# S5 preparation in a hybrid decoder trunk: C A^k B of four groups as four matmuls on column strips, one copy out, D added in one operation

## The chip, the cores and the metric

The kernel runs on one NeuronCore of a Trainium2 chip. The metric is the device time of one execution in microseconds (us), lower is better. TensorE (PE, its weight loads PEld), VectorE (DVE), ScalarE (ACT) and GpSimd (POOL) each work through their own instruction list in order; SyncE (SP) issues all transfers of this kernel, also in order.

## The reference, cut to what matters

Two layers over 512 tokens of width 1024. Each layer runs three token mixers on one input projection: Mamba-2 SSD (A), an S5 state space model (B) and latent attention, MLA (C). The change lies in B. S5 splits 1024 channels into 64 groups of 16 channels, each with 64 complex states:

```
bu = einsum('gph,bsgh->bsgp', bb, uf)          # input to states
x_t = abar * x_(t-1) + bu_t                    # diagonal, per group
y = Re(einsum('ghp,bsgp->bsgh', c, x)) + d_skip * uf
```

The kernel works in chunks of 8 tokens. Within a chunk y is a convolution of u with the 16x16 matrices C A^k B, k = 0 to 7, of each group, with the diagonal D added at k = 0.

## The kernel before, in words

Per layer, `layer` projects the input, then opens the pool `prep` and starts `s5_prep`, a generator. `mla` advances it by `fill` calls between its heads, so that S5 preparation (in lines: projections of u, powers of A, products) is spread over the 16 attention heads. After that come the S5 scan, SSD, the S5 blocks, the three merges and the output projection. A scheduler of the language puts each engine's instructions in order when the program is built, by times it assumes; the order is then fixed.

The head of `s5_prep` loads parameters and computes powers A^0 to A^8 (`ar`, `ai`) in many DVE operations on 128x64. It also loads D as `dT` (16 rows by 64 groups) and writes zeros to the first 112 columns of `kpad`, a buffer in DRAM which later holds the convolution matrices in a Toeplitz layout. `block(b)` handles eight groups: projection of u, a detour of u through DRAM (`ud`, eight `puf` transfers), loads of B and C (`bc`), then `q1` (name `pq`, on DVE) and the scaled B (`bb`, in the zero padded tile `pbb`) on POOL. `front` computes on POOL, for two groups, `w1` (name `pw`) and `v1` (name `pv1`, in a buffer of four groups, two buffers in all) and stores `v1` to `odr`. `back` runs one step behind: it transposes `w1` on PE into `pm`, splits that on ACT and DVE, and multiplies with u into `pM`. Every second step closes four groups:

- `pk`: one f32 matmul, B of four groups (4 x 32 columns, 16 of each 32 in use) as stationary operand, `v1` of the same four groups (4 x 128 columns) as moving operand. Of the 4 x 4 blocks of the result only the diagonal ones are used.
- four ACT copies of one 16x128 block each into `kf` (name `pkf`), rows 0 to 15.
- on POOL, `dd` (name `pdd`) = identity times `dT`, then `kf` += `dd` on 16 columns of each group.
- one transfer of `kf` into `kpad`.

There are 16 such closings per layer, 32 in all. The tiles `pm` and `pk` share one PSUM bank (tag `pb`).

Of the kernel before, what the change touches and what calls it, by code (L numbers as in the profile page):

```python
# [9 lines left out]
F32 = mybir.dt.float32  # L10
# [3 lines left out]
ALU = mybir.AluOpType  # L14
# [6 lines left out]
P = 128  # L21
# [13 lines left out]
class Trunk:  # L35
# [109 lines left out]
    def constants2(self):  # L145
        nc, c = self.nc, self.const
        for name, n in (("sgn", 2), ("ones", P), ("utri", P), ("cosT", 512), ("sinT", 512), ("cmask", 512)):
            t = c.tile([P, n], F32, name=name)
            nc.sync.dma_start(t, self.a[name])
            setattr(self, name, t)  # L150
        self.sel = c.tile([64, 16], F32R, name="sel")
        self.tt(self.sel, self.ident[0:64, 0:16], self.ident[0:64, 32:48], ALU.add)

# [81 lines left out]
    def s5_prep(self, l, pp):  # L235
        nc, a = self.nc, self.a
        pt = lambda nm, shape, bufs=1: pp.tile(shape, F32, name=nm, tag=nm, bufs=bufs)
# [46 lines left out]
        for h in range(2):  # L284
            q, g = slice(64 * h, 64 * h + 64), slice(32 * h, 32 * h + 32)
# [1 line left out]
            nc.vector.tensor_copy(sc1[q, 1], ar[q, 8, g])  # L287
            self.ts(sc2[q, 0], ai[q, 8, g], -1.0, None, ALU.mult)
            nc.vector.tensor_copy(sc2[q, 1], ai[q, 8, g])
        dT = pt("dT", [16, 64])  # L290
        nc.sync.dma_start(dT, a["s5_dT"][l])
        zero = pp.tile([16, 112], F32, name="zero", tag="pkf")
        nc.vector.memset(zero, 0.0)
        d = lambda nm, shape: self.dr.tile(shape, F32, name=f"{nm}{l}")
        kpad, odr, msd, u2 = d("kpad", [16, 64, 240]), d("odr", [P, 64, P]), d("msd", [2, 64, 2, 32, 64]), d("u2", [8, P, 512])
# [5 lines left out]
        et = self.gt  # L301
        pf = lambda nm: pp.tile([P, 512], F32, name=nm, tag="pf", bufs=2)

        bbp = [pt(f"pbb{i}", [P, 8, 32]) for i in range(2)]
# [54 lines left out]
        def back(b, s, uf, bb, v1, w1):  # L359
            if s == 0:  # L360
                u = keep["u"] = pp.tile([P, 8, 2, 64], F32R, name="pu2", tag="pu2")
                self.split(uf.rearrange("p (g c) -> p g c", g=8), u[:, :, 0], u[:, :, 1])
                keep["mo"] = pf("pmo").rearrange("p (g c) -> p g c", g=8)
                nc.gpsimd.memset(keep["mo"][:, :, 0], 0.0)
            u, mo = keep["u"], keep["mo"]
            pm = self.pq.tile([P, 512], F32, name="pm", tag="pb")
            for i in range(NB):
                nc.tensor.transpose(pm[:, i * P:i * P + P], w1[:, i].rearrange("p k h -> p (k h)"), self.ident)
            mh, ml = (pp.tile([P, NB * P], F32R, name=x, tag=x) for x in ("pmh", "pml"))
            self.split(pm[:, :NB * P], mh, ml)  # L370
            if s % 2 == 0:
                keep["pM"] = self.pq.tile([P, 4, 2, 64], F32, name="pM", tag="pM")
            pM = keep["pM"]
            for i in range(NB):
                g = NB * s + i
                k = slice(i * P, (i + 1) * P)
                nc.tensor.matmul(pM[:, g % 4], mh[:, k], u[:, g], start=True, stop=False)
                nc.tensor.matmul(pM[:, g % 4, 0], ml[:, k], u[:, g, 0], start=False, stop=True)
            if s % 2:
                q = 4 * (s // 2)  # L380
                self.act_(mo[:, q:q + 4, 1:64], pM[:, :, 0, 0:63])
                self.tt(mo[:, q:q + 4, 1:64], mo[:, q:q + 4, 1:64], pM[:, :, 1, 0:63], ALU.add)

                pk = self.pq.tile([P, 4, P], F32, name="pk", tag="pb")
                nc.tensor.matmul(  # L385
                    pk.rearrange("p g k -> p (g k)"), bbp[b % 2][:, q:q + 4].rearrange("p g h -> p (g h)"),
                    v1[:, :, 0:8].rearrange("p g k h -> p g (k h)"), start=True, stop=True,
                )
                kf = pt("pkf", [16, 4, P])
                for i in range(4):  # L390
                    self.act_(kf[:, i], pk[32 * i:32 * i + 16, i])
                g4 = slice(8 * b + q, 8 * b + q + 4)
                dd = pt("pdd", [16, 4, 16])
                et(
                    dd, self.ident[0:16, 0:16].unsqueeze(1).broadcast_to([16, 4, 16]),
                    dT[:, g4].unsqueeze(2).broadcast_to([16, 4, 16]), ALU.mult,
                )
                et(kf[:, :, 0:16], kf[:, :, 0:16], dd, ALU.add)
                nc.sync.dma_start(kpad[:, g4, 112:240], kf)
            if s == 3:  # L400
                nc.sync.dma_start(msd[b // 4, :, :, 8 * (b % 4):8 * (b % 4) + 8].rearrange("p r g c -> r p g c"), mo)

        todo = None
        for b in range(8):
            blk = block(b)
            yield
            for s in range(4):
                vw = front(b, s, *blk)
                if todo:
                    back(*todo)  # L410
                todo = (b, s, blk[0], blk[1], *vw)
                yield
        back(*todo)


# [811 lines left out]
```

## Time and profile before

| | |
|---|---|
| median of 3 runs | 2001.6 us (2001.11 to 2006.5) |
| the profiled execution | 1999.34 us, its span 1997.5 us |
| MLA with S5 preparation, layers 1 and 2 | about 90 to 400 us and 1080 to 1385 us |
| head of the preparation | about 20 to 90 us and 1019 to 1080 us |
| busy: PE, DVE, ACT, POOL | 1883.4, 1448.1, 941.1, 645.6 us |
| `pk` on PE | 64 MATMUL instructions for 32 calls, first at 91.4, last at 1375.8 us |

A chain is the sequence of work that ended last, followed back from the end; a share of it says where shorter work could shorten the run. A median duration of a PE matmul includes the flight through the array, so matmuls overlap in the list; the chain counts each only for the time until the next one follows.

### The profile page before, as it was taken

To read this page: it belongs to the slowest core of one execution; us is meant where nothing else is said; L and a number is where in the kernel's file an instruction comes from. 1 tells how busy PE (TensorE), PEld (TensorE's weight loads), DVE (VectorE), ACT (ScalarE), POOL (GpSimd) and SP (SyncE) were. 2 spreads that over 40 slices of the span, in tenths; PEclk is the share of its full clock that TensorE was granted. 3 is DMA by queue.
4 is the path that set the end of the run, shared out by engine and by line. 5 is a ranking of instruction groups with operands and counts; after the bars stand their busy time and mean duration, and the time that the engine had idled before them with its cause. 6 is when DMAs were issued, how large, how long until landed. Compare 5 with 4: busy or idle time off the path is not lost.

```text
span 1997.5 us, 27806 instructions
## 1 busy us (share of the span) xinstructions
PE 1883.4 (94%) x9688; PEld 1530.5 (77%) x9688; DVE 1448.1 (72%) x2845; ACT 941.1 (47%) x1743; POOL 645.6 (32%) x743
## 2 busy tenths in 40 slices
PE   7897999899999989999998999998999999999998
PEld 5685777687887778888876777776878887788887
DVE  6866667699999857744579666677999996666443
ACT  4364556522555545543333655564235563555431
POOL 1855467301233201201118556672013331012010
PEclk9898999899999999999998999998999999899999
DMA  5333244232312266345223333342232224662541
GB/s 159 94 115 86 88 116 121 74 120 81 131 64 73 70 172 182 106 132 177 96 84 88 112 104 111 91 140 83 96 122 78 75 74 111 182 173 85 166 130 42
DMA packets 132605, 219.96 MB, mean 110 GB/s; under 512 B 36208, under 2 KB 75760, under 8 KB 131952
## 3 DMA queue, kind: packets, MB, share of 16 engines
q1 hardware_dynamic: 132464, 218.19, 36.0%
q8 instruction: 76, 1.25, 0.2%
q14 instruction: 65, 0.53, 0.1%
HBM read 182.08 MB, written 31.33 MB: 107 GB/s over the span
## 4 chain that ended last, share of the span: by engine, by line
PE 59%; DVE 24%; DMA 8%; POOL 3%; ACT 3%; issue 2%; SPq 1%; DVEq 0%; POOLq 0%; ACTq 0%
PE mm L116 13%; PE mm L117 13%; PE mm L119 12%; DVE wl L78 4%; DMA wf<-in_w_in 3%; DVE keep L69 3%; PE mm L61 2%; PE mm L62 2%; PE mm L63 2%; DVE ms L894 2%; DVE sc_t L891 2%; PE pk L385 2%; DVE ms L893 1%; PE aux L61 1%; PE aux L62 1%
## 5 line engine op out<-in xcount | busy, mean ns | idle before, releaser
L116 PE MATMUL mm<-hh,wh 128*128 128x512 f32 (+1 forms) x1232 | 500.9, 407 | 16.0 <-DVE ql L78 8.8
L117 PE MATMUL mm<-hl,wh 128*128 128x512 f32 (+1 forms) x1232 | 493.5, 401 | 0.0
L66 ACT ACTIVATE wh<-wf 128x1024 fp32r<-128x1024 f32 (+1 forms) x294 | 291.4, 994 | 422.9 <-PE mm L117 232.7
L78 DVE TENSOR_TENSOR wl<-wf,wh 128x1024 fp32r<-128x1024 f32 (+1 forms) x243 | 297.0, 1227 | 180.6 <-ACT wh L66 151.9
L119 PE MATMUL mm<-hh,wl 128*128 128x512 f32 (+1 forms) x1232 | 315.4, 393 | 3.8 <-DVE wl L78 3.8
L116 PEld LDWEIGHTS mm<-hh,wh 128*128 128x128 f32 (+1 forms) x1232 | 237.3, 193 | 77.9 <-DVE ql L78 9.9
L117 PEld LDWEIGHTS mm<-hl,wh 128*128 128x128 f32 (+1 forms) x1232 | 236.7, 192 | 50.0 <-issue 1.9
L119 PEld LDWEIGHTS mm<-hh,wl 128*128 128x128 f32 (+1 forms) x1232 | 227.7, 187 | 53.3 <-DVE wl L78 4.6
L81 POOL TENSOR_TENSOR mg<-mg,tmp 128x512 f32<-128x512 f32 x32 | 77.4, 2420 | 461.4 <-DVE tmp L78 244.0
L81 POOL TENSOR_TENSOR wl<-wf,wh 128x1024 fp32r<-128x1024 f32 (+1 forms) x51 | 109.0, 2138 | 291.2 <-PE mm L119 185.9
L116 PE MATMUL mm<-ah,wh 128*128 128x512 f32 x512 | 200.6, 394 | 0.0
L117 PE MATMUL mm<-al,wh 128*128 128x512 f32 x512 | 199.8, 391 | 0.0
L119 PE MATMUL mm<-ah,wl 128*128 128x512 f32 x512 | 127.6, 390 | 0.0
L116 PEld LDWEIGHTS mm<-ah,wh 128*128 128x128 f32 x512 | 96.5, 189 | 21.6 <-issue 1.8
L117 PEld LDWEIGHTS mm<-al,wh 128*128 128x128 f32 x512 | 96.3, 188 | 20.6 <-DVE keep L78 0.5
L119 PEld LDWEIGHTS mm<-ah,wl 128*128 128x128 f32 x512 | 95.7, 188 | 19.5
L612 DVE CUSTOM_DVE_ANT_0 sc<-aux,cmask 128x128 f32<-128x128 f32 (+3 forms) x128 | 60.3, 485 | 50.2 <-PE aux L63 48.4
L81 POOL TENSOR_TENSOR pv<-pq,ar 128x288 f32<-128x288 f32 x64 | 56.7, 906 | 86.3 <-PE pk L385 69.8
L66 ACT ACTIVATE sc<-sc,nm 128x128 f32<-128x128 f32 (+3 forms) x128 | 70.3, 553 | 28.7 <-DVE nm L73 28.7
L78 DVE TENSOR_TENSOR pl<-aux,ph 128x512 fp32r<-128x512 f32 (+1 forms) x96 | 54.7, 593 | 25.6 <-ACT ph L66 25.2
L69 DVE SCALAR_TENSOR_TENSOR keep<-mm,cw,keep 128x511 f32<-128x511 f32 (+2 forms) x96 | 71.0, 740 | 2.1 <-ACT keep L66 1.5
L66 ACT ACTIVATE tmp<-mm 128x512 f32<-128x512 f32 x76 | 44.8, 593 | 58.5 <-PE mm L63 32.3
(344 smaller groups left out, 4083.4 us busy)
## 6 DMA issues: line engine op xcount, KB each, us to landing
wf<-in_w_in SPq DMA_DIRECT2D x156, 512.0 KB
odr<-pv SPq DMA_DIRECT2D x64, 128.0 KB
wf<-in_w_c SPq DMA_DIRECT2D x16, 512.0 KB
wf<-in_w_a SPq DMA_DIRECT2D x16, 512.0 KB
wf<-kpad SPq DMA_DIRECT2D x128, 64.0 KB
wf<-odr SPq DMA_DIRECT2D x16, 512.0 KB
wf<-in_w_glu SPq DMA_DIRECT2D x16, 512.0 KB
wf<-in_w_b SPq DMA_DIRECT2D x16, 512.0 KB
```

The lines of the kernel that those rows point to most:

```text
L61: mm(out, ah, bh, start=start, stop=False)
L62: mm(out, ah, bl, start=False, stop=False)
L63: mm(out, al, bh, start=False, stop=stop)
L66: self.nc.scalar.activation(out, in_, func, **kw)
L69: self.nc.vector.scalar_tensor_tensor(out, in0, s, in1, op0, op1)
L78: self.nc.vector.tensor_tensor(out, a, b, op)
L81: self.nc.gpsimd.tensor_tensor(out, a, b, op)
L116: mm(ps[:m], wh[:, o(i)], bh, start=i == 0, stop=False)
L117: mm(ps[:m], wh[:, o(i)], bl, start=False, stop=False)
L119: mm(ps[:m], wl[:, o(i)], bh, start=False, stop=i == k - 1)
L385: nc.tensor.matmul(pk.rearrange("p g k -> p (g k)"), bbp[b % 2][:, q:q + 4].rearrange("p g h -> p (g h)"), v1[:, :, 0:8].rearrange("p g k ...
L612: nc.vector.tensor_tensor_reduce(out=sc, in0=ps[:, :n], in1=self.cmask[:, 512 - n:512], op0=ALU.add, op1=ALU.max, scale=1.0, scalar=-3.0e3 ...
```

## The change

Four matmuls replace the one: the stationary operand of each is one group's 32 columns, the moving operand that group's 128 columns, and the result goes to 32 partitions of `pk` (`tile_position=(0, 32 * i)`, the i-th strip of 32 columns of the array). Now `pk` is 128x128 and holds only blocks that are used, one group to a strip. One ACT copy takes all of it. D is added on DVE by one operation for the four groups: `diag`, a constant with a 16x16 identity in each strip, times a column of `dT`, plus `kf`. For that `dT` becomes 128 rows by 16 columns, zeroed and filled by four transfers that pick every fourth group. `kf` goes to `kpad` in four transfers, one per group, and has two buffers.

```diff
+        self.diag = c.tile([P, 16], F32, name="diag")
+        self.tt(self.diag, self.ident[:, 0:16], self.ident[:, 32:48], ALU.add)
+        for i in (64, 96):
+            self.tt(self.diag, self.diag, self.ident[:, i:i + 16], ALU.add)
+        self.align(c, 48)
...
-        dT = pt("dT", [16, 64])
-        nc.sync.dma_start(dT, a["s5_dT"][l])
-        zero = pp.tile([16, 112], F32, name="zero", tag="pkf")
+        dT = pt("dT", [P, 16])
+        nc.vector.memset(dT, 0.0)
+        for i in range(4):
+            nc.sync.dma_start(dT[32 * i:32 * i + 16], a["s5_dT"][l].rearrange("h (n i) -> i h n", i=4)[i])
+        zero = pp.tile([16, 112], F32, name="zero", tag="pkf", bufs=2)
...
-                pk = self.pq.tile([P, 4, P], F32, name="pk", tag="pb")
-                nc.tensor.matmul(
-                    pk.rearrange("p g k -> p (g k)"), bbp[b % 2][:, q:q + 4].rearrange("p g h -> p (g h)"),
-                    v1[:, :, 0:8].rearrange("p g k h -> p g (k h)"), start=True, stop=True,
-                )
-                kf = pt("pkf", [16, 4, P])
+                pk = self.pq.tile([P, P], F32, name="pk", tag="pb")
                 for i in range(4):
-                    self.act_(kf[:, i], pk[32 * i:32 * i + 16, i])
-                g4 = slice(8 * b + q, 8 * b + q + 4)
-                dd = pt("pdd", [16, 4, 16])
-                et(
-                    dd, self.ident[0:16, 0:16].unsqueeze(1).broadcast_to([16, 4, 16]),
-                    dT[:, g4].unsqueeze(2).broadcast_to([16, 4, 16]), ALU.mult,
-                )
-                et(kf[:, :, 0:16], kf[:, :, 0:16], dd, ALU.add)
-                nc.sync.dma_start(kpad[:, g4, 112:240], kf)
+                    nc.tensor.matmul(
+                        pk[32 * i:32 * i + 32], bbp[b % 2][:, q + i], v1[:, i, 0:8].rearrange("p k h -> p (k h)"),
+                        start=True, stop=True, tile_position=(0, 32 * i),
+                    )
+                kf = pt("pkf", [P, P], 2)
+                self.act_(kf, pk)
+                n = 2 * b + s // 2
+                self.stt(kf[:, 0:16], self.diag, dT[:, n:n + 1], kf[:, 0:16], ALU.mult, ALU.add)
+                for i in range(4):
+                    nc.sync.dma_start(kpad[:, 8 * b + q + i, 112:240], kf[32 * i:32 * i + 16])
```

The scheduler sets the order anew, and rows move on every engine; three places matter below. The first is SP's list at the head of the preparation in the second layer, before:

```order
L242 DMA lim<-in_lim 64x64
L243 DMA ls<-in_log_step 128x64
L291 DMA dT<-in_s_dT 16x64
L297 DMA kpad_10372<-zero 1024x1x112
L323 DMA bc_10608<-in_s_bc 128x256
L324 DMA bc_10609<-in_s_bc 64x256
```

And the same place of the change, with the line numbers of the changed file:

```order
L248 DMA lim<-in_lim 64x64
L249 DMA ls<-in_log_step 128x64
L300 DMA dT<-in_s_dT 16x16x1 x4
L306 DMA kpad_10401<-zero 1024x1x112
L332 DMA bc_10637<-in_s_bc 128x256
L333 DMA bc_10638<-in_s_bc 64x256
```

The loads of B and C now stand behind four `dT` transfers of 256 single elements each, in place of one of 16 rows. The second place is DVE's list at the same time, where `pq` needs the first of these loads, before:

```order
L69 SCALAR_TENSOR_TENSOR e_p<-e_p,e_r 128x64 x3
L73 TENSOR_SCALAR pq_10615<-bc_10608,sgn 128x128
L69 SCALAR_TENSOR_TENSOR e_p<-e_p,e_r 128x64 x3
L69 SCALAR_TENSOR_TENSOR e_out<-e_p,e_t 128x64
L78 TENSOR_TENSOR p_z<-lre,e_out 128x64
L78 TENSOR_TENSOR p_ang<-lim,e_out 128x64
L75 TENSOR_SCALAR e_zc<-p_z 128x64
L75 TENSOR_SCALAR e_t<-e_zc 128x64
```

And of the change:

```order
L69 SCALAR_TENSOR_TENSOR e_p<-e_p,e_r 128x64 x6
L69 SCALAR_TENSOR_TENSOR e_out<-e_p,e_t 128x64
L78 TENSOR_TENSOR p_z<-lre,e_out 128x64
L78 TENSOR_TENSOR p_ang<-lim,e_out 128x64
L75 TENSOR_SCALAR e_zc<-p_z 128x64
L75 TENSOR_SCALAR e_t<-e_zc 128x64
L73 TENSOR_SCALAR pq_10644<-bc_10637,sgn 128x128
```

Here `pq` has moved behind eight small operations; in the first layer it moves behind one (`e_nf`). The third place is POOL's list early in the first layer, in the block after the first two closings, before:

```order
L81 TENSOR_TENSOR pv_1530<-pq_1397,ar 128x288 x2
L81 TENSOR_TENSOR pv_1530<-pv_1530,pv_1531 128x288
L81 TENSOR_TENSOR pkf<-pkf,pdd 16x4x16
L81 TENSOR_TENSOR pw_1532<-pbb_758,ar 128x256
L81 TENSOR_TENSOR pv_1566<-bc_1391,ai 128x288
L81 TENSOR_TENSOR pdd<-ident,dT 16x64
L81 TENSOR_TENSOR pw_1532<-pw_1532,pw_1533 128x256
```

And of the change:

```order
L81 TENSOR_TENSOR pv_1540<-pq_1407,ar 128x288 x2
L81 TENSOR_TENSOR pv_1540<-pv_1540,pv_1541 128x288
L81 TENSOR_TENSOR pw_1542<-pbb_767,ar 128x256
L81 TENSOR_TENSOR pv_1577<-bc_1401,ai 128x288
L81 TENSOR_TENSOR pw_1542<-pw_1542,pw_1543 128x256
```

The two small operations are gone from between `pv` and `pw`, and with them POOL's wait for the four ACT copies.

## Rows read from the trace of the kernel before

**Rows 1.** The page: busy us, share of span, instructions; chain by engine.

```profile
PE 1883.4 (94%) x9688; PEld 1530.5 (77%) x9688; DVE 1448.1 (72%) x2845; ACT 941.1 (47%) x1743; POOL 645.6 (32%) x743
...
PE 59%; DVE 24%; DMA 8%; POOL 3%; ACT 3%; issue 2%; SPq 1%; DVEq 0%; POOLq 0%; ACTq 0%
```

**Rows 2.** Windows: length; PE, PEld, DVE, ACT, POOL busy; clock, DMA share, GB/s.

```profile
90.00:400.00 310.00, 278.06 (x1383) 223.67 (x1382) 207.34 (x418) 173.75 (x424) 171.16 (x252) 0.91 0.35 100
...
1080.00:1385.00 305.00, 280.86 (x1395) 225.26 (x1395) 211.47 (x422) 173.36 (x426) 182.49 (x263) 0.92 0.35 102
```

**Rows 3.** The chain by line, of 90 to 400 us, then of 1080 to 1385 us.

```profile
by line: PE mm L116 13.9%; PE mm L117 13.3%; PE mm L119 12.2%; PE pk L385 4.8%; DVE keep L78 4.5%; PE aux L634 3.6%; POOL pv L81 3.2%; PE mm L61 3.1%; PE mm L62 2.9%; PE aux L645 2.7%; PE mm L63 2.7%; DVE sc L612 2.6%; DMA msd<-pmo 2.5%; PE
...
by line: PE mm L116 12.6%; PE mm L117 12.2%; PE mm L119 11.3%; PE pk L385 5.2%; PE aux L634 3.5%; POOL pv L81 3.1%; DMA wf<-in_w_in 3.0%; DVE keep L78 3.0%; SPq L316 2.6%; PE aux L61 2.6%; PE aux L62 2.2%; PE aux L63 2.2%; PE mm L61 2.1%; D
```

**Rows 4.** Pieces of the chain in order of time: start us, us, what.

```profile
165.65 0.95 PE pk L385 x2
...
166.67 1.28 POOL pv L81 x2
...
170.13 0.73 POOL pkf L81
...
171.51 0.70 POOL pdd L81
...
325.57 0.44 PE aux L634 x4
...
332.43 1.87 PE pk L385 x2
```

**Rows 5.** What touches pk: ns min/median/max, first and last start; who waited.

```profile
L385 PE MATMUL pk<-pv,pbb x64: 590/676/1202, 91.4 to 1375.8; 128*128 128x512 f32 x64
...
  POOL pv L81: 69.8, 23
```

**Rows 6.** A wl matmul of 128x512: by form (mean ns), and eight on the chain.

```profile
L119 PE MATMUL mm<-hh,wl 128*128 128x512 f32 x134 | 36.1, 396 | 0.0
...
104.60 1.82 PE mm L119 x8
```

**Rows 7.** What touches pkf (one row of waits), and pdd.

```profile
L66 ACT ACTIVATE pkf<-pk x128: 248/269/275, 95.6 to 1377.7; 16x128 f32<-16x128 f32 x128
L81 POOL TENSOR_TENSOR pkf<-pkf,pdd x32: 306/311/763, 96.7 to 1378.2; 16x64 f32<-16x64 f32 x32
L399 SPq DMA_DIRECT2D kpad<-pkf x32: 303/416/1273, 97.5 to 1378.5; - x32
...
  ACT pkf L66: 33.4, 6
...
L81 POOL TENSOR_TENSOR pdd<-ident,dT x32: 282/283/787, 21.1 to 1367.9; 16x64 f32<-16x64 f32 x32
```

**Rows 8.** By form, count, busy us and mean ns: an ACT copy from PSUM, a small DVE operation.

```profile
L66 ACT ACTIVATE pmh<-pm 128x256 fp32r<-128x256 f32 x30 | 11.4, 380 | 8.0 <-PE pm L368 7.7
...
L69 DVE SCALAR_TENSOR_TENSOR e_p<-e_p,e_r 128x64 f32<-128x64 f32 x12 | 2.7, 225 | 0.4
```

**Rows 9.** Waits of the whole run: waiter, releaser, us, times, longest.

```profile
DVE pml L78 <- ACT pmh L66: 13.9, 12, 3.3
```

**Rows 10.** Chain at both preparation heads, and DVE's pq with its idle time.

```profile
20.55 7.06 DMA bc<-in_s_bc
...
1019.04 6.99 DMA bc<-in_s_bc
...
1026.06 0.29 DVE L73 TENSOR_SCALAR pq<-bc,sgn 128x128 f32<-128x128 f32 x1 [2.25 <-DMA bc<-in_s_bc]
```

**Rows 11.** Windows of 1 us: kpad zeros being written, then puf transfers being loaded.

```profile
1022.00:1023.00 1.00, 0.94 (x8) 0.95 (x9) 1.00 (x5) 0.00 (x0) 0.00 (x0) 1.00 0.72 84
...
1073.00:1074.00 1.00, 0.00 (x0) 0.00 (x0) 1.00 (x2) 0.00 (x0) 1.00 (x2) 1.00 0.31 69
```

## The prediction

> **What bounds the kernel now.** I read the page first: PE is busy 94% of the span and holds 59% of the chain, DVE 24%, POOL and ACT 3% each [rows 1]. The change sits where MLA and S5 preparation run together, so I cut the run there: 310 and 305 us, in which PE is busy 278 and 281 us, ACT 174 and 173, POOL 171 and 182, DVE 207 and 211 [rows 2]. No engine is full, and the granted clock is 0.91 and 0.92, so PE pauses at times; but the chain by line in these stretches is led by PE's matmuls, and `pk` stands fourth with 4.8% and 5.2% [rows 3]. That is 14.9 + 15.9 = 30.8 us of chain for 32 calls, almost one full 0.95 us each [rows 4]. This is the number to watch: `pk` is a visible part of what ends last. It is also what releases others. POOL waits 69.8 us in 23 cases for `pk`, because the third `pv` buffer is the first one again, which `pk` must have read [rows 5]; behind that wait POOL runs a burst in which `pkf` and `pdd` themselves stand on the chain [rows 4].
>
> **The PE term.** One call is two MATMUL instructions of 512 columns [rows 5], 0.95 us on the chain, in some calls 1.87 [rows 4]. The new call is four matmuls of 128 columns, I take it as eight instructions, two of each strip. A 128 column f32 matmul costs 0.44 / 4 = 0.11 us on the chain [rows 4], so eight in a row cost 0.88 us: the same columns pass, and nothing is won unless strips work at once. No row shows strips. The bounds: none overlap, 0.88, which I take as no gain; all four overlap, 2 x 0.11 = 0.22, a gain of 77% of 30.8, or 23.6 us. In the order of the list the second instruction of a strip cannot run with the first of its own, but can with the first of the next strip; that gives five steps, 0.55 us, a gain of 0.39 / 0.95 = 41%, or 12.6 us. I take this one.
>
> The strips are another shape of the array, and before and after each group whatever is in flight may have to leave first. The row for it is a 128x512 matmul: 396 ns from start to end, while eight of them advance the chain by 1.82, or 0.227 each [rows 6], so 0.17 us of flight is hidden today. Exposed twice in each of 32 calls it is 10.9 us; exposed never, 0. I take half, 5.4 us, since one of the two exposures could be covered by the eight short instructions. The Trainium skill, page TensorEngine Tiling (Array Packing), section Tiling Modes, says that changing the tiling mode drains TensorE; by that rule the whole 10.9 us would be paid, and the sum below would be 5.5 us worse. No run here shows it yet; a rival below has the case worked out from rows.
>
> **ACT.** Four copies of 0.269 us become one [rows 7]. The one copy has 128 columns as each of the four had, on 128 partitions; a copy of 256 columns on 128 partitions takes 0.380 [rows 8], so it lies between 0.269 and 0.380. At 0.27 the saving is 3 x 0.269 x 32 = 25.8 us of ACT. ACT has 3% of 1997.5 = 60 us on the chain out of 941 busy [rows 1], 6.4%; so 1.6 us. Bounds: 0 to 25.8.
>
> **POOL.** `pkf` and `pdd` go: (0.311 + 0.283) x 32 = 19.0 us, and so do 33.4 us of waiting for the ACT copies [rows 7], in which everything behind on POOL's list waited. By POOL's share of the chain (60 of 646 us, 9.3%) it is 1.8 us; all of it would be 52. In one burst the two take 0.73 + 0.70 = 1.43 us on the chain [rows 4]; I take four such bursts among 32 closings, 6 us.
>
> **DVE.** It gains 32 operations on 128x16. The nearest row is 0.225 us for 128x64 [rows 8], so 7.2 us, of which DVE's share of the chain (24% of 1997.5 over 1448, 33% [rows 1]) makes 2.4. Each waits for an ACT copy, with the whole of DVE's list behind it, weight splits and softmax maxima included. The like pair, `pml` behind `pmh`, runs 64 times (four steps, eight blocks, two layers) and costs 13.9 us of waiting [rows 9]; 32 such pairs would cost 7, of which 33% is 2.3. Such waits partly replace others, so I take 3 in all, bounds 0 to 4.7. The three operations for `diag` run while DVE would wait for `bc` anyway, and the memset of `dT` is one small operation per layer: nothing.
>
> **SP.** 96 more `kpad` issues of 0.416 us [rows 7] are 40 us of SP, and the loads of weights and rope rows queue behind them. SP has 1% of the chain [rows 1]; 5% of 40 is 2 us. Bounds 0 to 40. `kpad` is read only by the S5 blocks, which come after the scan and SSD, so its own landing costs nothing.
>
> **The head of the preparation.** This is what speaks most against the change. In both layers the chain runs through the landing of `bc`, 7.06 and 6.99 us, and DVE idles 2.25 us for it in the second [rows 10]. Ahead of `bc` in the queue stand 1024 packets of `kpad` zeros: at 84 GB/s and 448 B that is 188 packets per us on 0.72 x 16 engines, 61 ns each; a `puf` packet of 256 B costs by the same sum 0.31 x 16 / 270 = 18 ns [rows 11]. Now 1024 packets of 4 B stand there too, 64 per engine: 3.9 us at 61 ns, 1.2 at 18, and not less than three more issues, 3 x 0.416 = 1.2 us. I take `bc` 2.5 us later, between the ends. In the first layer `pq` moved by one operation (0.2 us), so 2.3 us; in the second eight operations now run first, 8 x 0.225 = 1.8 us [rows 8], so 0.7. Together 3 us, bounds 1 to 6; it goes on the chain whole, because everything behind `pq` on DVE (the powers of A) is on it.
>
> **The sum.** -12.6 + 5.4 - 1.6 - 6 + 3 + 2 + 3 = -6.8 us. Against the profiled execution, 1999.3 us, that is 1992.5; the median of the runs is 2.3 us above it, so I forecast 2001.6 - 6.8 = 1994.8 us. A measurement of this kernel can tell about 0.3%, 6 us, from no change, so 1995.6 to 2007.6 counts as the same.
>
> **Rivals.** All strips at once and no pause: the PE term is -23.6, the others stand, sum -23.2, 1978.4 us. For it speaks only that the strips share no column; against it the pairs of instructions. The Trainium skill, page TensorE: Matmul & The Clock Gate, Part 3 on packing small matmuls, gives 2.38 times the speed for three column strips; that would be 0.40 us a call, between this case and the forecast, and no run here shows it.
>
> Pairs of strips, but both pauses in every call: PE -12.6 + 10.9, sum -1.3, 2000.3 us. For it: the 0.17 us of flight are real today [rows 6]; against it: eight short instructions may cover one of the two.
>
> Slower: strips run one after the other and each call pays both pauses, 0.88 + 0.34 = 1.22 us in place of 0.95: PE +10.9, sum +11.1, 2012.7 us. It decides as soon as a call takes over about 0.95 us, since the other terms nearly cancel (+0.4). For it: no row shows any two f32 matmuls at once; against it: in the rows the flight of one matmul always runs beside the next, so two do share the array in time.
>
> The gain moves on: `pk` is shorter, but POOL's burst and DVE's list behind it end as late as now, because POOL starts at `pk`'s end and the burst itself is longer than `pk`. PE's term is then nothing and the rest is +0.4: 2002.0 us. For it: PE is busy only nine tenths there [rows 2]. Slow `dT` packets (more than 61 ns) end in the same place.
>
> The new order is better by itself: POOL no longer blocks, its burst is shorter, and transposes start earlier in more than four closings; twelve such would be 17 us in place of 6, 1984 us.
>
> **Chances.** Forecast 0.45, its own range 1988 to 2001; of it 0.25 below 1995.6. All strips 0.15; the better order 0.08; pairs with both pauses 0.07; the gain moves on 0.12; slower 0.13. So faster 0.25 + 0.15 + 0.08 = 0.48, same 0.20 + 0.07 + 0.12 = 0.39, slower 0.13. The range leaves out half of the all-strips case and most of the slower one: 1979 to 2008 us.
>
> **What would show it.** In the changed profile: starts of the `pk` instructions 0.11 us apart without overlap mean no strips at once, two together mean pairs; the distance from the last `pk` to the next matmul shows the pause. `pk` on the chain should fall from 30.8 us to about 18 to 24. POOL's wait for ACT `pkf` should be gone, and a wait of DVE for it should appear, under 10 us. `bc` should land 2 to 3 us later behind its issue, and DVE idle at `pq` longer. The prediction is wrong if `pk` takes over 0.95 us per call, if `dT` delays `bc` by over 5 us, or if the new order sets other loads late.

## The result and the profile after

| | median | range | runs |
|---|---|---|---|
| before | 2001.36 us | 2000.85 to 2006.5 | 4 |
| after | 1976.54 us | 1974.83 to 1978.56 | 4 |

The ratio is 0.9871, 95% interval 0.9851 to 0.9891: faster by 1.3%, some 25 us. The forecast of 1994.8 us was 18 us too high, and the time lies below the range (1979). The profiled execution took 1977.92 us.

The page of the changed kernel, busy time by engine and the chain by engine (compare [rows 1]):

```profile
PE 1870.3 (95%) x9880; PEld 1528.1 (77%) x9880; DVE 1420.3 (72%) x2882; ACT 914.2 (46%) x1647; POOL 631.9 (32%) x679
...
PE 60%; DVE 22%; DMA 9%; ACT 3%; issue 2%; POOL 2%; SPq 2%; DVEq 0%; ACTq 0%; POOLq 0%
```

The span fell from 1997.5 to 1976.1 us, 21.4 us. PE's busy time fell by 1883.4 - 1870.3 = 13.1 us, so its idle time (span less busy) fell by 8.3 us, from 114.1 to 105.8. These two numbers are used for every kernel below. Each is from one execution: e7 and e13 below have the very PE list of the changed kernel, and their busy times are 1863.6 and 1868.1 us, their idle times 109.6 and 110.9. So differences of up to 7 us busy and 5 us idle between two kernels tell nothing by themselves.

What touches `pk`: duration min/median/max in ns, first and last start, form (compare [rows 5, 7]); under it who waited for it.

```profile
L395 PEld LDWEIGHTS pk<-pv,pbb x256: 106/109/154, 93.8 to 1358.4; 128*32 128x32 f32 x128
L395 PE MATMUL pk<-pv,pbb x256: 272/297/423, 93.8 to 1358.6; 128*32 128x128 f32 x128
L66 ACT ACTIVATE pkf<-pk x32: 258/272/322, 96.4 to 1359.4; 128x128 f32<-128x128 f32 x32
...
  POOL pv L81: 68.7, 19
```

A call is indeed eight MATMUL instructions (256 for 32 calls), and the one copy takes 0.272 us, no more than each of the four small ones. POOL's wait for `pk` is as long as before (68.7, was 69.8). `pk` on the chain fell from 30.8 us to 2.0 + 4.7 us in 5 + 12 pieces; most are like this one:

```profile
159.90 0.35 PE pk L395 x8
```

Stretches of the whole run, cut at the first load of each preparation and at the first load of the S5 scan; columns as in [rows 2]. First the kernel before:

```profile
18.10:397.20 379.10, 340.97 (x1694) 275.34 (x1694) 264.04 (x579) 197.25 (x461) 208.39 (x299) 0.91 0.35 99
397.20:1017.20 620.00, 605.48 (x3195) 494.67 (x3194) 463.92 (x846) 275.53 (x414) 113.74 (x71) 0.99 0.37 115
1017.20:1383.70 366.50, 334.12 (x1653) 266.60 (x1653) 263.95 (x575) 192.99 (x457) 212.74 (x299) 0.93 0.35 101
1383.70:1997.50 613.80, 597.07 (x3129) 489.16 (x3127) 448.01 (x822) 266.46 (x390) 108.04 (x65) 0.99 0.36 113
```

The same for the changed kernel:

```profile
16.70:387.50 370.80, 337.57 (x1798) 275.22 (x1796) 253.08 (x598) 185.04 (x414) 201.65 (x267) 0.93 0.35 102
387.50:1005.30 617.80, 603.21 (x3189) 494.08 (x3187) 462.71 (x846) 274.44 (x414) 112.40 (x71) 0.99 0.38 115
1005.30:1367.40 362.10, 330.32 (x1756) 267.59 (x1754) 252.03 (x599) 181.07 (x410) 206.48 (x267) 0.92 0.36 102
1367.40:1976.10 608.70, 594.24 (x3125) 487.01 (x3124) 444.29 (x815) 264.70 (x390) 108.89 (x65) 0.99 0.37 114
```

The two stretches that hold the change (the first and the third) are shorter by 8.3 and 4.4 us; of these 12.7 us PE's busy time makes 3.4 + 3.8 = 7.2. The remaining 8.7 us lie in the second and fourth stretch (2.2 and 5.1) and before the first (1.4), where none of the new matmuls runs. Not all of this is time won there. PE's counts in the first and third stretch rose by 104 and 103, and the new matmuls are 96 of each, so 15 others moved in over the cuts. And kernels with the same PE list differ by as much as the second stretch did: it lasts 619.1 us in e7 and 616.2 in e13, the fourth 607.9 and 609.5, the first 366.6 and 370.6.

**The price of a call.** PE's timeline around one call, before: start us, duration us, what.

```profile
165.40 0.25 PE L378 MATMUL pM<-pu,pml 128*128 128x64 f32 x1
165.48 1.10 PE L385 MATMUL pk<-pv,pbb 128*128 128x512 f32 x2
166.02 0.79 PE L116 MATMUL mm<-hh,wh 128*128 128x512 f32 x1
166.65 0.40 PE L117 MATMUL mm<-hl,wh 128*128 128x512 f32 x1
```

And after, with the same neighbours:

```profile
159.65 0.25 PE L387 MATMUL pM<-pu,pml 128*128 128x64 f32 x1
159.83 0.42 PE L395 MATMUL pk<-pv,pbb 128*32 128x128 f32 x8
160.18 0.50 PE L116 MATMUL mm<-hh,wh 128*128 128x512 f32 x1
160.52 0.40 PE L117 MATMUL mm<-hl,wh 128*128 128x512 f32 x1
```

Ends are modelled, so starts are what to read. From the start of the matmul ahead to the start of the second one behind it was 1.25 us and is 0.87, a saving of 0.38 us a call, or 12.2 us for 32. Pauses on both sides are in these rows: the call starts 0.18 us behind its neighbour where it was 0.08, and L116 keeps L117 waiting 0.34 us where a step of this kind takes 0.23 [rows 6]. That is 0.10 and 0.11 us. A third part is in the call itself, which takes 0.35 us where two steps of 0.11 (priced below) are 0.22. Without any of them the 0.87 us would be 0.08 + 0.22 + 0.23 = 0.53, so the pauses are 0.34 us a call, 10.9 us in all.

The eight instructions start in two sets of four. The same view, from 159.82 to 159.85, has four of them in it:

```profile
159.83 0.32 PE L395 MATMUL pk<-pv,pbb 128*32 128x128 f32 x4
```

The other four start from 159.96 to 159.98 in the trace.

### The profile page after: what moved, and what is told of

It is laid out like the page before. It is cut to its first block, busy times and chain, and to the rows that moved or that the text cites. A ratio compares the mean times of both kernels' runs of the same rounds, so it can differ in the third digit from the quotient of the medians.

```text
span 1976.1 us, 28153 instructions
## 1 busy us (share of the span) xinstructions
PE 1870.3 (95%) x9880; PEld 1528.1 (77%) x9880; DVE 1420.3 (72%) x2882; ACT 914.2 (46%) x1647; POOL 631.9 (32%) x679
## 4 chain that ended last, share of the span: by engine, by line
PE 60%; DVE 22%; DMA 9%; ACT 3%; issue 2%; POOL 2%; SPq 2%; DVEq 0%; ACTq 0%; POOLq 0%
PE mm L116 15%; PE mm L117 14%; PE mm L119 14%; DMA wf<-in_w_in 3%; DVE wl L78 3%; DVE keep L69 3%; PE mm L61 2%; PE mm L62 2%; PE mm L63 2%; PE aux L61 1%; DVE tmp L69 1%; DVE ms L899 1%; PE aux L62 1%; PE aux L63 1%; DVE sc_t L896 1%
## 5 line engine op out<-in xcount | busy, mean ns | idle before, releaser
L116 PE MATMUL mm<-hh,wh 128*128 128x512 f32 (+1 forms) x1232 | 499.5, 405 | 11.5 <-ACT wh L66 8.0
L117 PE MATMUL mm<-hl,wh 128*128 128x512 f32 (+1 forms) x1232 | 492.0, 399 | 0.0
L116 PEld LDWEIGHTS mm<-hh,wh 128*128 128x128 f32 (+1 forms) x1232 | 236.5, 192 | 72.2 <-ACT wh L66 11.6
L117 PEld LDWEIGHTS mm<-hl,wh 128*128 128x128 f32 (+1 forms) x1232 | 236.2, 192 | 48.5 <-issue 0.5
L116 PE MATMUL mm<-ah,wh 128*128 128x512 f32 x512 | 200.3, 393 | 0.0
L117 PE MATMUL mm<-al,wh 128*128 128x512 f32 x512 | 199.9, 391 | 0.0
L116 PEld LDWEIGHTS mm<-ah,wh 128*128 128x128 f32 x512 | 96.2, 188 | 21.4 <-ACT pkf L66 0.7
L117 PEld LDWEIGHTS mm<-al,wh 128*128 128x128 f32 x512 | 96.1, 188 | 20.9 <-issue 1.0
L81 POOL TENSOR_TENSOR pv<-pq,ar 128x288 f32<-128x288 f32 x64 | 49.1, 789 | 77.2 <-PE pk L395 68.7
L81 POOL TENSOR_TENSOR pw<-pbb,ar 128x256 f32<-128x256 f32 x64 | 51.0, 799 | 41.8 <-PE pm L377 41.6
```

The source lines that it names most:

```text
L81: self.nc.gpsimd.tensor_tensor(out, a, b, op)
L116: mm(ps[:m], wh[:, o(i)], bh, start=i == 0, stop=False)
L117: mm(ps[:m], wh[:, o(i)], bl, start=False, stop=False)
```

## The experiments

All times are medians, of 4 to 12 executions, against the kernel before on the same chip; the kernel before had medians of 1999.4 to 2001.6 us there. A thousandth of the ratio is 2 us. PE busy and idle are from the profiled execution, which in e3, e6 and e15 was 8.3, 3.8 and 6.7 us faster than the median.

| run | what it is | median us | ratio, interval | PE busy, idle us |
|---|---|---|---|---|
| before | | 2001.4 | | 1883.4, 114.1 |
| after | | 1976.5 | 0.9871 [0.9851, 0.9891] | 1870.3, 105.8 |
| e1 | before + strips | 1993.1 | 0.9947 [0.9932, 0.9961] | 1869.1, 122.7 |
| e2 | e1, all in one strip | 1998.8 | 0.9984 [0.9972, 0.9996] | 1890.5, 108.5 |
| e3 | after, old matmul, four copies | 2008.9 | 1.0031 [1.0018, 1.0043] | 1874.3, 124.5 |
| e4 | after, D on POOL | 1981.6 | 0.9890 [0.9872, 0.9907] | 1863.8, 116.8 |
| e5 | after, four copies | 1985.9 | 0.9923 [0.9910, 0.9937] | 1861.8, 120.3 |
| e6 | after, strips twice | 1982.3 | 0.9902 [0.9887, 0.9916] | 1863.6, 112.8 |
| e7 | after, D in rows of 64 B | 1977.9 | 0.9882 [0.9868, 0.9896] | 1863.6, 109.6 |
| e8 | e7, `bc` first | 1977.1 | 0.9879 [0.9864, 0.9895] | 1865.5, 105.9 |
| e9 | e5, one strip | 2013.2 | 1.0069 [1.0049, 1.0088] | 1888.1, 126.0 |
| e10 | e5, two strips | 1998.7 | 0.9994 [0.9979, 1.0009] | 1878.0, 123.1 |
| e13 | after, one `pkf` buffer | 1980.6 | 0.9898 [0.9883, 0.9913] | 1868.1, 110.9 |
| e14 | e5, D on POOL, one buffer | 1983.2 | 0.9911 [0.9897, 0.9926] | 1863.9, 117.4 |
| e17 | e1, four transfers | 1996.4 | 0.9968 [0.9953, 0.9983] | 1873.6, 125.3 |
| e18 | e14, one strip | 1976.5 | 0.9873 [0.9856, 0.9889] | 1877.3, 97.3 |
| e11 | before, other order | 2247.5 | 1.1250 [1.1226, 1.1274] | 1979.0, 266.7 |
| e12 | after, other order | 2229.7 | 1.1149 [1.1126, 1.1172] | 1973.6, 256.2 |
| e15 | e1, other order | 2209.8 | 1.1039 [1.1013, 1.1065] | 1952.1, 248.9 |
| e16 | e5, other order | 2211.1 | 1.1056 [1.1033, 1.1079] | 1960.2, 246.1 |

PE's busy time also holds the granted clock. The calls of `pk` that take 1.87 us of chain before, in place of 0.95 [rows 4], stand where the granted clock is 0.50 (1.2 in place of 2.4 GHz), as this window of the kernel before shows (columns as in [rows 2]):

```profile
332.50:334.20 1.70, 1.70 (x3) 0.67 (x4) 1.67 (x5) 0.87 (x2) 0.00 (x0) 0.50 0.79 272
```

If each microsecond of busy time counts by the clock granted in it (1 or 0.5 in the trace), PE's work comes out as 1826.2 us before and 1814.1 after, 12.1 us less. The kernels with four strips (e1, e4, e5, e7, e8, e13, e14, e17) have 1812.7 to 1816.0, those with one strip (e2, e9, e18) 1831.3 to 1834.0. This is an estimate, good to some 6 us: e3, with the matmuls of the kernel before, has 1832.3.

### Strips alone, and the same in one strip

The kernel before with this edit, and the copies reading `pk[32 * i:32 * i + 16]`; everything else is old.

```diff
-                pk = self.pq.tile([P, 4, P], F32, name="pk", tag="pb")
-                nc.tensor.matmul(...)
+                pk = self.pq.tile([P, P], F32, name="pk", tag="pb")
+                for i in range(4):
+                    nc.tensor.matmul(
+                        pk[32 * i:32 * i + 32], bbp[b % 2][:, q + i], v1[:, i, 0:8].rearrange("p k h -> p (k h)"),
+                        start=True, stop=True, tile_position=(0, 32 * i),
+                    )
```

e1. 

> The kernel before with the four matmuls on strips alone; four ACT copies, D on POOL, one transfer to kpad and the old load of D stay. Theory PE (the strips run at once, and a call costs TensorE 0.35 us in place of 0.95): 32 x 0.60 = 19 us less than before, so 1980 to 1985 us. Rival POOL (the gain comes from taking D and its wait off POOL): 1998 to 2002 us, no change. Rival order (the gain is luck of the new order): anywhere from 1990 to 2005.

e2 has `tile_position=(0, 0)` for all four, and `pk` as 32 rows by four groups. 

> As e1, but all four matmuls use the first strip, and their results lie side by side on 32 partitions. The same number of matmuls and weight loads, so only the overlap of strips is taken away. Theory PE: a call costs 8 x 0.11 = 0.88 us plus the pauses at its ends, 0.9 to 1.2 us, so 2000 to 2010 us. Rival: if the gain of the strips is only that the weight load is smaller or the order luckier, it stays at about 1980 to 1990.

Measured: 8.5 us less with strips, 2.8 less in one strip. PE's busy time fell by 14.3 us in e1, more than in the change, but its idle time rose by 8.6. So the strips save their PE time in the old surroundings too (weighted by the clock 10.8 us); how much of it arrives at the end is left open by the interval, which allows 7.8 to 13.6 us.

### The change without strips, and with D on POOL

e3 keeps the old single matmul and four copies in the changed kernel; e4 replaces the one DVE operation.

```diff
-                self.stt(kf[:, 0:16], self.diag, dT[:, n:n + 1], kf[:, 0:16], ALU.mult, ALU.add)
+                dd = pt("pdd", [P, 16])
+                et(dd, self.diag, dT[:, n:n + 1].broadcast_to([P, 16]), ALU.mult)
+                et(kf[:, 0:16], kf[:, 0:16], dd, ALU.add)
```

e3. 

> The changed kernel with the one old matmul, and four ACT copies of 32x128 into the four strips of kf; D on DVE, four transfers and the new load of D stay. Theory PE: the whole gain is lost, 1997 to 2003 us. Rival POOL: most of it stays, 1978 to 1986 us.

e4. 

> The changed kernel with D multiplied and added on POOL, in two operations on 128x16, in place of one on DVE. Theory PE: within 4 us of the changed kernel, 1974 to 1981 us. Rival POOL: most of the gain is lost, 1990 to 2000 us.

Measured: without strips and with four copies the rest of the change makes the kernel slower than before, by 0.3%. D on POOL costs 5 us on the medians, but the intervals of e4 and of the change overlap.

### Four copies, a second set of matmuls, and dT

```diff
-                self.act_(kf, pk)
+                for i in range(4):
+                    self.act_(kf[32 * i:32 * i + 32], pk[32 * i:32 * i + 32])
```

e5. 

> The changed kernel, with four ACT copies of 32x128, one for each strip, in place of the one copy of 128x128; everything else as in the change. Theory (the strips' matmuls run at the same time, and most of what the change won is PE's time at pk): three more copies of 0.27 us in 32 closings are 26 us of ACT, which is half idle, so 1977 to 1982 us, ratio 0.988 to 0.990. Rival (what counts is that one copy frees pk's bank and lets the list behind it go on 0.8 us sooner in each closing): 32 x 0.8 = 26 us, of which at least half shows: 1990 to 2000 us, ratio 0.994 to 0.999.

e6 runs the loop over the strips with `for i in (0, 1, 2, 3, 0, 1, 2, 3)`. 

> The changed kernel, with the four strip matmuls issued twice in each closing into the same place (the second set writes the same values again). It prices a call on its own. Theory (all four strips at once, 0.35 us a call on the chain): where pk is on the chain (6.7 of 32 x 0.35 = 11.2 us) a second set costs as much, 5 to 11 us: 1982 to 1988 us, ratio 0.990 to 0.993. Rival (the strips work in pairs or one after the other, and the chain hides it): 0.55 to 0.88 us for each second set, 18 to 28 us in 32 closings: 1994 to 2005 us, ratio 0.996 to 1.002.

Measured: four copies cost 9.3 us, though their 26 us are on an engine that is half idle; in the profiled executions PE was idle 14.5 us longer and busy 8.5 us less; the latter goes with the clock, for weighted it is 1814.5 us against 1814.1. The second set costs 5.7 us, with intervals that overlap a little. The chain of e6 shows what a set adds: where all 16 instructions stand in one piece it is 0.57 us long, 0.21 more than a single set.

```profile
161.87 0.36 PE pk L395 x8
...
211.90 0.57 PE pk L395 x16
```

e7 and e8 leave every list of the changed kernel as it is, except for a handful of rows (none on PE, ACT and POOL in e7, some ten on PE in e8, which moves loads on SP besides), so they tell of the load alone.

```diff
-            nc.sync.dma_start(dT[32 * i:32 * i + 16], a["s5_dT"][l].rearrange("h (n i) -> i h n", i=4)[i])
+            nc.sync.dma_start(dT[32 * i:32 * i + 16], a["s5_dT"][l, i])
...
-    d["s5_dT"] = c(i["s5_d"].reshape(L, 64, 16).transpose(0, 2, 1))
+    d["s5_dT"] = c(i["s5_d"].reshape(L, 16, 4, 16).transpose(0, 2, 3, 1))
```

e7. 

> The changed kernel, with D laid out by the host in such an order that the four dT transfers take 16 rows of 64 B in place of 256 single elements of 4 B; the order on the engines is nearly the same. Theory (the single elements delay bc by about 1 us in each layer, and bc is on the chain): 1974 to 1976 us, ratio 0.986 to 0.988. Rival (packets of 4 B cost as much as I put into the prediction's upper bound, 3 us a layer): 1970.5 us, ratio 0.9845. Second rival (hidden): 1976.5 us.

e8 moreover issues these transfers and the zeros of `kpad` behind the loads of `bc`. 

> As the kernel with D in rows of 64 B, and the dT transfers and the kpad zeros are issued after the first block's loads, so that bc no longer stands behind them. Theory (bc's landing of 7 us is on the chain at both heads, of which some 3 us are the packets ahead of it): 2 x 2 to 3 us less: 1969 to 1973 us, ratio 0.9835 to 0.986. Rival (the order that the scheduler makes anew moves more than that): anything from 1965 to 1990 us; then the time at the two heads in the trace tells what bc won, and the rest of the difference lies elsewhere.

Measured: neither moves the time. In the changed kernel the second layer's `pq` waits for `bc` (DVE's timeline; `ls`, the step it is counted from, was issued at 1005.25):

```profile
1016.24 0.29 DVE L73 TENSOR_SCALAR pq<-bc,sgn 128x128 f32<-128x128 f32 x1 [2.62 <-DMA bc<-in_s_bc]
```

In e8, with `ls` issued at 999.08, it no longer does:

```profile
1003.44 0.29 DVE L73 TENSOR_SCALAR pq<-bc,sgn 128x128 f32<-128x128 f32 x1
```

That is 11.0 us behind `ls` against 4.4: 6.6 us earlier, in the first layer 7.0 (12.07 against 5.08). Before, it was 9.6 and 8.8. So the change did delay `bc`, by 2.5 and 2.2 us, as forecast, and undoing that delay three times over brings nothing. e7 by itself brings `pq` 0.9 and 0.8 us forward behind `ls` (11.15 and 10.18 us), as its theory had it, and nothing of this shows either.

### One, two and four strips

e9 and e10 are e5 with the strip of a matmul changed to 0, and to `32 * (i % 2)`.

e9. 

> The kernel with four strip copies (1985.9 us), but all four matmuls of a closing go to the same column strip, one behind the other, into four places of the bank. Nothing else changes. Theory (the gain at pk is that the strips run at the same time): eight instructions of 0.11 us in a row, 0.88 us in place of 0.35, so 32 x 0.53 = 17 us of PE, of which half to all shows: 1994 to 2003 us, ratio 0.997 to 1.001. Rival (the gain comes from fewer columns for each instruction and the smaller weights, not from strips at once): 1984 to 1989 us.

e10. 

> The same with two column strips, the four matmuls going to them in turn. Theory: two strips halve the row of eight, about 0.44 to 0.5 us a call against 0.35 and 0.88, so it stands 3 to 5 us above four strips: 1988 to 1991 us, ratio 0.993 to 0.995. Rival (pairs are all that the array overlaps, as the prediction had it): the same time as four strips, 1984 to 1987 us.

Pieces of the chain, two strips (some of its eight records are missing), then one strip; four strips are shown above.

```profile
161.22 0.55 PE pk L395 x6
```

```profile
242.06 0.99 PE pk L395 x8
```

In the timeline, two strips:

```profile
160.97 0.25 PE L387 MATMUL pM<-pu,pml 128*128 128x64 f32 x1
161.15 0.62 PE L395 MATMUL pk<-pv,pbb 128*32 128x128 f32 x6
161.70 0.50 PE L116 MATMUL mm<-hh,wh 128*128 128x512 f32 x1
```

And one strip:

```profile
241.82 0.25 PE L387 MATMUL pM<-pu,pml 128*128 128x64 f32 x1
242.00 1.06 PE L395 MATMUL pk<-pv,pbb 128*32 128x128 f32 x8
242.99 1.19 PE L119 MATMUL mm<-hh,wl 128*128 128x512 f32 x4
```

Counted from start to start, from the 128x64 matmul ahead to the first matmul behind, a call takes 0.53 us in four strips (159.65 to 160.18), 0.73 in two (160.97 to 161.70) and 1.17 in one (241.82 to 242.99). 0.35, 0.55 and 0.99 on the chain are 0.11 us for each instruction that a strip has to take (2, 4 or 8) and 0.12 us besides. So the strips do work at once, all four, and within a strip the instructions follow one another. The whole times rose too, by 12.8 and 27.3 us, more than the calls' 32 x 0.20 = 6.4 and 32 x 0.64 = 20.5.

### Another order

Four of these kernels, unedited but for the language's simpler way of setting the order:

```diff
-    with tile.TileContext(nc, schedule_with_timeline_sim=True) as tc:
+    with tile.TileContext(nc, schedule_with_timeline_sim=False) as tc:
```

e11. 

> The kernel before, with the language's other way of setting the order at build (a scheduler without its simulated timeline). Every engine's list comes out in another order. It is here to be compared with the next run; no theory says where it stands against the kernel before: 2000 to 2080 us.

e12. 

> The changed kernel in that other order. Theory (most of the 25 us is work and waiting that the change itself takes away): it stands 15 to 30 us under the previous run, 0.985 to 0.9925 of it. Rival (the order that came out with the change was a lucky one): under 10 us from the previous run, 0.995 to 1.005 of it.

e15, strips alone. 

> The kernel before with strips alone, in the other order (compare with 2247.5 us of the kernel before and 2229.7 of the changed kernel in that order). Theory (a call saves 0.6 us of PE whatever stands around it, 32 x 0.6 = 19 us, of which half or more shows): 2230 to 2238 us. Rival (strips alone give little without the one copy, as in the first order, where they gave 8.5 of 24.9): 2239 to 2245 us.

e16, four copies. 

> The changed kernel with four strip copies in place of one, in the other order. Theory (the one copy frees pk's bank 0.8 us sooner and gives 26 us of ACT back, of which a third shows, as in the first order): 2236 to 2241 us. Rival (the 9.3 us were that order's): 2228 to 2233 us.

Measured: the order alone makes the kernel before 12.5% slower (e11). The whole change is worth 17.8 us here, strips alone 37.7, four copies and all the rest 36.4. The parts that were worth 17 us in the first order (e1 to after) cost 20 in this one, and the one copy, 9.3 us to the good there, is 18.6 to the bad.

### One buffer; three parts undone; the transfers; and one strip again

e13, `kf = pt("pkf", [P, P])`, the same lists on every engine. 

> The changed kernel with one pkf buffer in place of two. Theory (strips and the one copy carry the gain; a second buffer helps little, because closings are some 18 us apart): 1976 to 1980 us, ratio 0.987 to 0.989. Rival (with one buffer the next copy waits until the four kpad transfers have read pkf, about 2 us, and that is what held back the strips alone): 1985 to 1993 us, ratio 0.992 to 0.996.

e14. 

> The changed kernel with three of its parts undone at once: D added on POOL by two operations on 128x16, four copies of 32x128, one pkf buffer. Left of the change are the strips, the smaller kf of 128x128, four transfers and the four dT transfers. Theory (each undone part costs what it cost alone, 9.3 for the copies and 5.0 for POOL): 1990 to 1993 us, as the kernel with strips alone, ratio 0.995 to 0.996. Rival (the parts overlap, or the strips alone only met a bad order): 1982 to 1987 us.

e17, e1 with four `kpad` transfers. 

> The kernel before with strips, as in the first experiment (1993.1 us), and four kpad transfers for each closing in place of one. Theory (transfers cost SP 40 us that hide, and what separates strips alone from the kernel with D on POOL, four copies and one buffer, 10 us, is where PE idles by the order): 1990 to 1996 us, ratio 0.9945 to 0.9975. Rival (one transfer of four groups holds pkf longer than four small ones, so POOL and ACT wait for it): 1982 to 1987 us, ratio 0.991 to 0.993.

e18, e14 in one strip. 

> The kernel with D on POOL, four copies and one buffer in the new layout (1983.2 us), with all four matmuls of a closing in the same column strip. It prices the strips a third time, in other surroundings than the first two pairs. Theory (a call is 0.64 us longer on PE, 32 calls, 20 us, and all of it shows as in the pair before): 2000 to 2012 us, ratio 0.9995 to 1.0055. Rival (with POOL waiting for the copies the strips' gain is mostly hidden, as in the kernel before, 5.7 us): 1987 to 1992 us.

Measured: the second buffer is worth 4 us at most; the intervals overlap. Undone one by one the three parts cost 9.3, 5.0 and 4.1 us, together only 6.7. Transfers alone change e1 by 3 us to the worse, as the theory had it.

e18 is the surprise. Its matmuls take 0.99 us a call, and it is 6.7 us faster than e14 and as fast as the change. The page of e18:

```profile
PE 1877.3 (95%) x9880; PEld 1538.2 (78%) x9880; DVE 1406.5 (71%) x2850; ACT 939.0 (48%) x1743; POOL 644.8 (33%) x743
```

PE is busy 13.4 us longer than in e14 (1863.9), as it must be, but idle for 97.3 us, the least of all. By stretches, first e14, the two that hold the preparation:

```profile
17.80:388.90 371.10, 337.11 (x1808) 273.37 (x1806) 250.89 (x585) 200.61 (x465) 212.60 (x299) 0.94 0.35 102
...
1007.20:1374.20 367.00, 330.21 (x1762) 267.34 (x1762) 250.21 (x587) 195.25 (x460) 210.27 (x299) 0.93 0.35 101
```

and e18:

```profile
16.50:398.20 381.70, 351.69 (x1835) 287.71 (x1834) 252.84 (x594) 199.64 (x466) 211.50 (x299) 0.94 0.34 99
...
1013.50:1367.00 353.50, 329.71 (x1754) 270.25 (x1753) 244.40 (x579) 193.28 (x457) 208.20 (x299) 0.95 0.36 105
```

In the first layer e18 pays for its one strip, 10.6 us. In the second it gains 13.5 us: PE is idle 23.8 us in place of 36.8, and the granted clock is 0.95 in place of 0.93. Of PE's waits in that stretch of e14 (waiter, releaser, us, times, longest) two rows

```profile
PE aux L61 <- DVE mx L620: 6.7, 4, 4.8
...
PE aux L61 <- DMA qh<-rrh: 4.0, 2, 2.7
```

have no or nearly no counterpart in e18:

```profile
PE aux L61 <- DMA qh<-rrh: 0.3, 1, 0.3
```

The scores matmuls of attention (L61) wait for a softmax maximum and for rope rows. Neither has anything to do with `pk`; they stand elsewhere in the lists. And POOL, which adds D in e18, waits for the ACT copies there as long as it did before (33.4 us [rows 7]):

```profile
POOL pkf L81: 32.7, 4
```

Of what had been expected of these runs, the theory held in e6 and e12, and a rival in e1, e7, e8 and e14; e2, e4, e13 and e17 came out at most 1.2 us outside the theory's range. e3, e5, e9, e10, e11, e15, e16 and e18 lie outside every range given for them.

## Why the prediction was wrong

**The rest of the sum, priced in the old lists, is the step that failed most.** I took PE's term as -7.2 us net and everything else as +0.4, and gave "the new order is better by itself" 8% and 11 us. Measured, the 32 calls are 12.2 us shorter, and PE's work, weighted by the clock, is 12.1 us less. The other half of the 25 us is in the rest, where I had +0.4: PE idled 8.3 us less in the profiled executions. Among the kernels in the first order PE's idle time runs from 97 to 126 us, a spread of 29 us. e9 and e18 differ only in who adds D and in the second buffer, parts that are worth 5.0 and 4.1 us the other way by e4 and e13. PE's weighted work is 1834.0 us in both, and yet they stand at 2013 and 1976 us. e18 has neither the four strips nor the one copy, D on DVE or the second buffer, and is as fast as the change, so none of these four parts is needed to come to this time.

Of three single parts undone the effects don't add up (e4, e5, e13 against e14); in the other order their sign turns (e15, e16 against e12). Seven pairs differ in little more than strips: before and e1, before and e17, e2 and e1, e3 and e5, e9 and e5, e18 and e14, e11 and e15; strips give 8.5, 4.1, 5.7, 23.0, 27.3, -6.7 and 37.7 us. So that strips shorten PE's work is shown; how much of the 25 us they are is not. About half, 12 us, is the size of what PE's rows lost. The other half I put down to waiting that came out shorter with this order; this is argued and not shown. That order alone can do it is shown by e11, which changes nothing else and moves the kernel before by 12.5%. Which rows made it so in the change stays open: its lists differ from the old ones in too many places at once.

**Strips: pairs.** I argued that the second instruction of a strip can run only with the first of the next one, five steps, 0.55 us. The first half holds, the second doesn't: e9, e10 and e5 give 0.11 us for each instruction of one strip and no waiting between strips, so two steps and the pauses, 0.35 us on the chain. The rival "all strips at once and no pause", 1978.4 us, comes within 2 us of the result, but by the sum and not by its reasons: it has no pause, and its PE term of 23.6 is twice what PE's rows show. All strips at once with both pauses in full, -23.6 + 10.9 = -12.7, is what they show, and no case of mine had it. (The rival "slower" is added up wrongly: 1.22 us in place of 0.95 is 8.6 us in 32 calls, not 10.9, and 10.9 + 0.4 would be 11.3, not 11.1.) `pk` on the chain did fall by 24.1 us, as that rival had it; but the chain is one path among near ties, and work taken out of it uncovers the next.

**The pauses** come to 0.34 us a call, 10.9 us in 32 calls, against the 5.4 I took: nothing covers them. With one and with two strips it is nearly the same: up to the first matmul behind the call 0.21 us (1.17 less 0.08 and eight steps of 0.11; 0.73 less 0.08 and four steps), against 0.23 with four, and the second one follows 0.33 and 0.34 us later (243.32 and 162.04). The Trainium skill, page TensorEngine Tiling (Array Packing), section Tiling Modes, says that changing the tiling mode drains TensorE; the trace agrees, with a pause on each side, and with the 0.34 us that I worked out from the flight of the 128x512 matmul. Put together, the call went from 1.25 to 0.87 us, 12.2 us in all, where the net term was 7.2.

**ACT.** One copy of 128 partitions takes 0.272 us, as taken. What the saved 26 us are worth is not shown: in e5 the three copies more cost 9.3 us where I took 1.6, in the other order they gain 18.6. A wait that would fit is there, since PE's transposes `pm`, which share `pk`'s bank, wait for `pkf`'s copies 14.7 us on PE and 8.9 on PEld in e5, 9.9 and 5.4 in the change. But the kernel before, with four copies, has only 4.3 and 0.6 us of it.

**POOL and DVE.** POOL's wait for the ACT copies is gone, and DVE's wait for `pkf`'s copies is not among those who waited for them, so my +3 for DVE finds no support as a wait. The operation itself is dearer than I took: its median is 0.608 us, not 0.225. POOL's term of -6 agrees with e4 (5.0 us, intervals that overlap), but e14, with D on POOL and one buffer, is no slower than e5, and e18 has POOL's wait back and is as fast as the change; so the term is not shown.

**The head.** `bc` came 2.2 to 2.5 us later behind `ls`, as forecast. That this goes on the chain whole is wrong: e8 brings `pq` 7 us forward in both layers, with PE's list all but the same, and gains nothing. The reason that I gave, everything behind `pq` on DVE is on the chain [rows 10], is true of the path that ended last, and says nothing of the one just behind it. **SP** is as harmless as it can be told: e17 adds 96 issues to e1 and comes out 3 us later, within the intervals.

## What to carry to other kernels

A change that makes a scheduler order all lists anew draws a new lot: here two kernels with almost the same work (e9, e18) came out 37 us apart, so the price of an edit in the old lists is one term, the new order another of its size, and the range has to hold both. To learn what an edit does, read PE's busy and idle time apart, against what the granted clock does to both and what two kernels of the same list differ by, and look for variants that leave the lists as they are (other data layout, another buffer count, a load moved); only those gave clean prices here. A long piece at the head of the chain is no promise: take it away by an experiment before paying or booking it.

## What the hardware showed

- f32 matmuls with 128x32 weights and 128 moving columns overlap wholly in different strips of 32 columns: eight instructions take 0.35 us in four strips, 0.55 in two, 0.99 in one, and a second set of eight adds 0.21 us. The Trainium skill, page TensorE: Matmul & The Clock Gate, Part 3 on packing small matmuls, gives 2.38 times for three column strips; the rows here show 0.99 / 0.35 = 2.8 for four.
- Entering and leaving the strips costs 0.31 to 0.34 us a call in all, whether the call uses four strips or one. A weight load of 128x32 takes 109 ns.
- Four `dT` transfers of 256 single elements were issued in 2.6 us and landed in 2.3; in rows of 64 B in 1.7 to 1.8 and 1.6.
- In e18's second layer 13 us less of PE idle time went with a granted clock of 0.95 in place of 0.93, and PE was busy no longer than in e14, though its calls took 0.64 us more.
